# Order of the mixers' small matrix products on TensorE, in a two-layer hybrid encoder

## Chip, cores and metric

The kernel runs on one core of one Trainium2 chip. The metric is the device time of one execution in microseconds (us), as the median of several runs. Each profile is one execution taken by the hardware profiler.

## What is computed

The input x is 512 tokens of 1024 features in float32. Two layers follow each other; each adds half a SwiGLU feed-forward block, a token mixer, and again half a feed-forward block, each behind an RMS norm. The mixer computes four branches from one projection of the normalised input, weighs them with sigmoid gates and projects the sum:

```python
p = u @ w_in
p_da, p_gla, p_ssd, p_rw, p_gate = split_cols(p, MIXER_COLS)
...   # A: differential attention, 4 heads x 2 score maps, 64 wide
y_a = differential_attention(q, k, v, lam, lam_init, da_norm)
...   # B: gated linear attention, 4 heads, chunks of 64 tokens
o = gla_chunked(q, k, v, log_g)
...   # C: Mamba-2 SSD, 8 heads, 2 groups, chunks of 64 tokens
y = ssd_chunked(xh, dt, A, bm, cm) + ssd_d[:, None] * xh
...   # D: RWKV-7, 8 heads of 64, a state of 64 x 64 per head
state = state * w_t + sa[..., None] * (kk_t * a_t) + v_t[..., None] * k_t
...
proj = jnp.einsum('bsnc,ncd->bsnd', ys, w_branch)
merged = jnp.sum(sigmoid(p_gate + gate_b) * proj, axis=2)
return merged @ w_out
```

## The kernel before

**Wide products.** Projections, feed-forward, gates, merges and output are products of 128 rows, 128 columns and 512 moving columns. Each is made of three float32r products of split operands (high x high, high x low, low x high): `mm3` at L164 to L166, `tok` at L201 to L203. A weight unit comes by a DMA on SP's queue into one of three buffers, and ScalarE and VectorE split it (L157, L159).

**The mixer.** `cotrace` traces two streams against each other, by estimated costs that the streams yield as (TensorE time, latency after it). One is RWKV-7 (`rwkv`); the other is attention (`diff_attn`), then `gla`, then `ssd`. Where TensorE would idle by the estimate, it traces filler: the 32 gates, then the merges of branches that are done. From the traced order, as priorities, and the dependencies a scheduler makes a fixed order for each engine. Every engine then works through its queue in that order.

**Small products.** The mixers' own products are float32. Their operands lie on 128, 64 or 32 partitions (the rows of the array), and their outputs on 128, 64 or 32 partitions (its columns). Chunks have 64 tokens, and a 128-partition tile holds two heads or two chunks, one in partitions 0 to 63 and one in 64 to 127. The lines that matter:
- L615 (`rwkv`, preparation): the chunk's 128 x 128 interaction matrices of one head, 64 rows, four chunks to an output tile; heads one after the other, each with its own "rs" tile, and VectorE's masking (through the helper at L81) behind each.
- L651: the products of those matrices with v, 64 x 64, eight chunks of one head, then of the other.
- L705 and L709: the 32 x 32 corrections of the triangular inverses, again head by head, with a negation on ScalarE (L707) between them.
- L735, L743, L749, L757 to L763: the chunk recurrence, four products each (two head pairs, two heads). A PSUM tile `step` holds all of a chunk's. The last two kinds share an accumulation and are kept in order by `chained`:

```python
last = self.chained(last, lambda: mm(
    out=o, lhsT=am[pl, h, hf][:, cc, 64:128], rhs=sav[hf][:, pl, cc, h, :], start=True, stop=c == 0))
if c:
    last = self.chained(last, lambda: mm(
        out=o, lhsT=ar[pl, hf][hp, cc, 1, :], rhs=state[hp, pl, :], start=False, stop=True))
```

- L719 turns the normalised output of a chunk pair, with heads in turn.
- L518 and L522: two projections of RWKV's low-rank parts, from partitions 0 to 63 and 64 to 127.
- L871 (`diff_attn`): the scores of one of a head's two maps, 64 rows, up to 512 keys; VectorE masks and reduces each before the next is traced. L885 and L891 are the transposes and the product with v.
- L1025 and L1031 (`gla`): per chunk four products with the state and four that make the next state; after each of the latter VectorE updates the state (L1033, L1035) from the same PSUM tile.
- L1154, L1163, L1168 (`ssd`): the products within the chunk (two chunks of a token tile one after the other), the products with the state, and those for the next state.

**PSUM.** `small(tag)` hands out tiles of one bank; the tags "pb", "rs", "os" and "oy" have two banks each. RWKV uses "rs", the other mixers "os", and "oy" for some outputs and for `tok`.

Of the kernel before, what the change touches and what calls it, by code (L numbers as in the profile page):

```python
# [73 lines left out]
class Body:  # L74
# [4 lines left out]
    # ---------------------------------------------------------------- helpers  # L79
# [22 lines left out]
    def rsqrt(self, y, a, pool, tag):  # L102
        """y = a ** -0.5 for normal positive a."""
# [14 lines left out]
    def rsqrt_neg_half(self, hm, pool):  # L118
        """a ** -0.5 for the [128, 1] tile hm = -a / 2."""
# [3 lines left out]
        # the shifted sign and the halved exponent are in the constant  # L123
# [6 lines left out]
    def keep(self, t):  # L130
        """0 at the chunks' starts, 1 elsewhere."""
        self.nc.gpsimd.memset(t, 1.0)
        self.nc.gpsimd.memset(t[:, 0:512:64], 0.0)
        return t

    @contextmanager
    def prio(self, d):
        """Issue what is traced within as if it were traced d instructions later."""
        self.tc.cur_priority += d
        yield  # L140
        self.tc.cur_priority -= d

    def chained(self, last, fn):
        """Issue the matmuls that fn traces behind the matmul last (order in one PSUM bank)."""
        if last is None:
            return fn()
        with self.tc.issue_after(last.ins):
            return fn()

    # ------------------------------------------------------------ weight units  # L150
# [17 lines left out]
    def feat(self, ap):  # L168
        """[128 features, 512 tokens] of the projection by one unit."""
# [7 lines left out]
    def feat2(self, aps):  # L177
        """Two units' projections, the first half of the tokens before the second."""
# [12 lines left out]
    def tok(self, units, lh, ll, tags=("pb", "pb", "oy", "oy"), tail=0):  # L191
        """Four [128 tokens, 512] products: stationary lh/ll (feature-major), moving the units.
        The last tail units go by token tile, so that the tiles end one after another."""
# [27 lines left out]
    # ------------------------------------------------------------------ norm  # L221
# [9 lines left out]
    def norm_(self, x, gain, pool, out=None, g=None):  # L231
        """RMS norm of x (tiles [t][half]); to xh/xl feature-major, or rows to out."""
# [6 lines left out]
        for t in range(NT):  # L239
            # hm = -(mean square + eps) / 2, the first half's part ahead of the second's  # L240
# [38 lines left out]
    # ------------------------------------------------------------------- ffn  # L279
# [26 lines left out]
    # ----------------------------------------------------------------- mixer  # L306
# [65 lines left out]
    def filler(self, yd, gd, es):  # L372
        """The gates, then the merges of the branches that are done."""
# [38 lines left out]
    def cotrace(self, streams, filler):  # L412
        """Trace the streams by their estimated times, the filler where TensorE would idle."""
# [52 lines left out]
    # ---------------------------------------------------------------- RWKV-7  # L466
    def rwkv(self, ydst):
# [34 lines left out]
        for ph in range(2):  # L502
# [5 lines left out]
            for pl in range(2):  # L508
# [26 lines left out]
                # decay of the state between the chunks' references  # L535
# [12 lines left out]
                # normalised key  # L548
# [20 lines left out]
                # k' = k (1 + (a - 1) k_a)  # L569
# [3 lines left out]
                # bonus  # L573
# [17 lines left out]
                for hf in range(2):  # L591
# [6 lines left out]
                    # rows of even heads hold [beta | kappa], of odd ones [kappa | beta]  # L598
# [12 lines left out]
                    for h in range(2):  # L611
                        hp = slice(64 * h, 64 * h + 64)
                        ps = self.small("rs", (128, 4, 128))
                        for j in range(4):
                            mm(  # L615
                                out=ps[:, j, :],
# [4 lines left out]
                            )  # L621
                        m = r2((128, 4, 128), name="am")
                        self.mul(m, ps, self.c("rwmask").unsqueeze(1).to_broadcast([128, 4, 128]))
# [9 lines left out]
                # v token-major: even heads on partitions 64..127, odd ones on 0..63  # L633
# [12 lines left out]
                # A(kappa, alpha) V  # L646
                pu = self.small("rs", (128, 8, 64))
                for h in range(2):
                    hp, vp = slice(64 * h, 64 * h + 64), slice(64 - 64 * h, 128 - 64 * h)
                    for c in range(NC):  # L650
# [7 lines left out]
            # inverses of the unit-triangular 32x32 diagonal blocks, a block per partition  # L658
# [39 lines left out]
            for pl in range(2):  # L698
# [3 lines left out]
                for h in range(2):  # L702
                    lo, hi = slice(64 * h, 64 * h + 32), slice(64 * h + 32, 64 * h + 64)
                    for c in range(NC):
                        mm(out=ps[hi, c, :], lhsT=am[pl, h, c // 4][lo, c % 4, 32:64], rhs=xt1[pl][lo, c, :],  # L705
                           start=True, stop=True)
                    self.act(qt[hi], ps[hi], AF.Copy, scale=-1.0)  # L707
                    for c in range(NC):
                        mm(out=ps2[lo, c, :], lhsT=qt[hi, c, :], rhs=tt[pl][hi, c, 32:64], start=True, stop=True)  # L709
                    nc.vector.tensor_copy(tt[pl][lo, :, 32:64], ps2[lo])  # L710
# [14 lines left out]
            # the chunks in turn  # L725
            state, late = None, None
            for c in range(NC):
# [19 lines left out]
                if c < NC - 1:  # L747
# [7 lines left out]
                    else:  # L755
                        self.mul(new, step[:, 2], fc)
                for pl, h, hp in heads:  # L757
# [584 lines left out]
```

## Time and profile before

| | |
|---|---|
| median of 3 runs | 3215.84 us (3211.01 to 3217.59) |
| span of the profiled execution | 3212.2 us, 40884 instructions |
| TensorE busy | 3147.8 us (98%) |
| weight loads busy (beside the matmuls) | 2499.3 us (78%) |
| VectorE busy | 1621.3 us (50%) |
| ScalarE busy | 1148.1 us (36%) |
| granted clock of TensorE over the span | 0.991 of full speed |

The busy time of an engine is the time in which at least one of its instructions runs. Matmuls are pipelined and their ends are modelled: a busy TensorE isn't one at its peak, and the time that one product costs is read from its start and the start of the next.

### The profile page before, as it was taken

The numbers are of one execution on the slowest core, as the hardware profiler recorded it, in microseconds if no ns is written. First come the engines' busy times: TensorE is split into PE (matmuls) and PEld (weight loads), VectorE is DVE, ScalarE is ACT, GpSimd is POOL, SyncE is SP. The second block draws the span as 40 slices with busy tenths as digits, with TensorE's granted clock in tenths as the row PEclk, the third lists the DMA queues.
The fourth block names the chain that finished last, engine by engine and source line by source line (L and its number), as shares of the span: only waits on it lengthen the run. The fifth ranks groups of instructions, "written<-read, shape, count | busy, mean of one in ns | idle before, by whom it ended". The sixth has DMA issues, their size and how long they took to land.

```text
span 3212.2 us, 40884 instructions
## 1 busy us (share of the span) xinstructions
PE 3147.8 (98%) x16160; PEld 2499.3 (78%) x16160; DVE 1621.3 (50%) x3310; ACT 1148.1 (36%) x1754; POOL 137.8 (4%) x160
## 2 busy tenths in 40 slices
PE   8999999999999999999999999999999999999998
PEld 6888787777777777888888888777777777778887
DVE  4332446756475775332343324567654757753323
ACT  3222245654432323222222223356553323232222
POOL 0000000000011100000000000000000011000000
PEclk9999999999999999999999999999999999999999
DMA  4222322322222543222332233223122215432222
GB/s 165 98 98 93 129 89 88 103 67 96 86 83 63 180 168 138 99 98 93 108 132 94 99 112 110 93 87 104 60 93 95 86 56 181 172 132 93 98 99 79
DMA packets 138592, 338.50 MB, mean 105 GB/s; under 512 B 35104, under 2 KB 43680, under 8 KB 137632
## 3 DMA queue, kind: packets, MB, share of 16 engines
q1 hardware_dynamic: 138400, 335.88, 30.8%
q8 instruction: 127, 2.08, 0.3%
q14 instruction: 65, 0.53, 0.1%
HBM read 297.55 MB, written 38.27 MB: 105 GB/s over the span
## 4 chain that ended last, share of the span: by engine, by line
PE 90%; DVE 7%; ACT 2%; issue 1%; DMA 0%; SPq 0%; DVEq 0%; ACTq 0%
PE pb L164 18%; PE pb L165 18%; PE pb L166 18%; PE oy L203 3%; PE oy L201 3%; PE oy L202 3%; PE pb L202 2%; PE pb L201 2%; PE pb L203 2%; PE rs L203 1%; PE os L203 1%; PE rs L201 1%; PE os L201 1%; PE os L202 1%; PE rs L202 1%; PE os L871 1%
## 5 line engine op out<-in xcount | busy, mean ns | idle before, releaser
L157 ACT CAST whi<-wraw 128x1024 fp32r<-128x1024 f32 x478 | 501.6, 1051 | 1479.6 <-PE pb L165 545.8
L159 DVE TENSOR_TENSOR wlo<-wraw,whi 128x1024 fp32r<-128x1024 f32 x466 | 571.7, 1227 | 894.5 <-ACT whi L157 880.8
L164 PE MATMUL pb<-xh,whi 128*128 128x512 f32 (+1 forms) x2448 | 957.0, 391 | 4.9 <-DVE rwr L97 2.7
L165 PE MATMUL pb<-xl,whi 128*128 128x512 f32 (+1 forms) x2448 | 949.5, 388 | 3.4 <-DVE xl L81 3.4
L166 PE MATMUL pb<-xh,wlo 128*128 128x512 f32 (+1 forms) x2448 | 949.6, 388 | 0.0
L164 PEld LDWEIGHTS pb<-xh,whi 128*128 128x128 f32 x2448 | 466.5, 191 | 110.2 <-issue 16.6
L165 PEld LDWEIGHTS pb<-xl,whi 128*128 128x128 f32 x2448 | 466.7, 191 | 95.8 <-issue 6.3
L166 PEld LDWEIGHTS pb<-xh,wlo 128*128 128x128 f32 x2448 | 467.0, 191 | 93.5 <-issue 6.1
L81 DVE TENSOR_TENSOR s<-s,pb 128x512 f32<-128x512 f32 x88 | 60.5, 688 | 286.9 <-PE pb L166 284.8
L100 ACT ACT_TABLE_LOAD x118 | 151.4, 1283 | 12.5 <-PE os L1141 9.7
L165 PE MATMUL pb<-yl,whi 128*128 128x512 f32 x256 | 102.1, 399 | 0.9 <-DVE yl L81 0.9
L164 PE MATMUL pb<-yh,whi 128*128 128x512 f32 x256 | 102.5, 403 | 0.0
L166 PE MATMUL pb<-yh,wlo 128*128 128x512 f32 x256 | 102.1, 399 | 0.0
L159 POOL TENSOR_TENSOR wlo<-wraw,whi 128x1024 fp32r<-128x1024 f32 x12 | 28.4, 2379 | 1318.3 <-ACT whi L157 1318.3
L202 PE MATMUL pb<-wlo,xh 128*128 128x512 f32 x192 | 76.7, 399 | 0.0
L201 PE MATMUL pb<-whi,xh 128*128 128x512 f32 x192 | 76.6, 399 | 0.0
L201 PE MATMUL oy<-whi,xh 128*128 128x512 f32 x192 | 76.0, 396 | 0.0
L203 PE MATMUL oy<-whi,xl 128*128 128x512 f32 x192 | 75.8, 395 | 0.0
L203 PE MATMUL pb<-whi,xl 128*128 128x512 f32 x192 | 75.8, 395 | 0.0
L202 PE MATMUL oy<-wlo,xh 128*128 128x512 f32 x192 | 75.3, 392 | 0.0
L201 PE MATMUL pb<-whi,hh 128*128 128x512 f32 x176 | 69.1, 392 | 0.0
L202 PE MATMUL pb<-wlo,hh 128*128 128x512 f32 x176 | 69.0, 392 | 0.0
(418 smaller groups left out, 4339.7 us busy)
## 6 DMA issues: line engine op xcount, KB each, us to landing
wraw<-in_ffn_gu SPq DMA_DIRECT2D x176, 512.0 KB, 3.2
wraw<-in_win_f SPq DMA_DIRECT2D x118, 512.0 KB, 3.3
wraw<-in_ffn_d SPq DMA_DIRECT2D x88, 512.0 KB, 3.2
wraw<-in_win_t SPq DMA_DIRECT2D x48, 512.0 KB, 3.3
gd<-sg SPq DMA_DIRECT2D x64, 256.0 KB, 2.1
wraw<-in_wbr SPq DMA_DIRECT2D x32, 512.0 KB, 3.4
msg<-gd SPq DMA_DIRECT2D x64, 256.0 KB, 3.0
wraw<-in_wout SPq DMA_DIRECT2D x16, 512.0 KB, 3.2
```

Of the source, the lines that this page charges most:

```text
L81: return (eng or self.nc.vector).tensor_tensor(out=out, in0=in0, in1=in1, op=op)
L100: return self.nc.scalar.activation(out=out, in_=in_, func=func, **kw)
L157: nc.scalar.copy(hi, raw)
L159: eng.tensor_tensor(out=low, in0=raw, in1=hi.bitcast(F32), op=ALU.subtract)
L164: mm(out=ps, lhsT=lh, rhs=rh, start=first, stop=False)
L165: mm(out=ps, lhsT=lh, rhs=rl, start=False, stop=False)
L166: return mm(out=ps, lhsT=ll, rhs=rh, start=False, stop=last)
L201: mm(out=pst[t], lhsT=lh(k)[:, lt], rhs=hi[:, c], start=k == 0, stop=False)
L202: mm(out=pst[t], lhsT=lh(k)[:, lt], rhs=low[:, c], start=False, stop=False)
L203: mm(out=pst[t], lhsT=ll(k)[:, lt], rhs=hi[:, c], start=False, stop=k == nk - 1)
L871: mm(out=s[:, 0:n], lhsT=qT[qb][cp_, h, :], rhs=kT[h][cp_, 0:n], start=True, stop=True)
```

## The change

In the mixers, loops around small products change places: products that lie next to each other in the traced order now use different halves of the array's rows or columns (two heads or two chunks in turn), and products of one shape are traced as a group. For that, L615 and the scores of L871 take two PSUM tiles at once, and the scores move from tag "os" to "oy". GLA goes by token tiles of two chunks, makes all products for the state first, then the updates, and then the products with the state; its yields change accordingly. SSD makes both chunks' products for the state, then the states, then the products with them. In the chunk recurrence the first group of products sets the start flag only for the first head pair of the tile. No operation is added or removed. Comments go, so later lines have other numbers.

```diff
-                    for h in range(2):
-                        hp = slice(64 * h, 64 * h + 64)
-                        ps = self.small("rs", (128, 4, 128))
-                        for j in range(4):
+
+                    pss = [self.small("rs", (128, 4, 128)) for _ in range(2)]
+                    for j in range(4):
+                        for h in range(2):
+                            hp = slice(64 * h, 64 * h + 64)
                             mm(
-                                out=ps[:, j, :],
+                                out=pss[h][:, j, :],
                                 lhsT=b[hp, j].rearrange("p s t -> p (s t)"),
                                 rhs=x[hp, j].rearrange("p s t -> p (s t)"),
                                 start=True,
                                 stop=True,
                             )
+                    for h in range(2):
                         m = r2((128, 4, 128), name="am")
-                        self.mul(m, ps, self.c("rwmask").unsqueeze(1).to_broadcast([128, 4, 128]))
+                        self.mul(m, pss[h], self.c("rwmask").unsqueeze(1).to_broadcast([128, 4, 128]))
...
-                for h in range(2):
-                    hp, vp = slice(64 * h, 64 * h + 64), slice(64 - 64 * h, 128 - 64 * h)
-                    for c in range(NC):
+                for c in range(NC):
+                    for h in range(2):
+                        hp, vp = slice(64 * h, 64 * h + 64), slice(64 - 64 * h, 128 - 64 * h)
                         mm(out=pu[hp, c, :], lhsT=am[pl, h, c // 4][vp, c % 4, 0:64],
                            rhs=sav[c // 4][vp, pl, c % 4, h, :], start=True, stop=True)
...
                 qt = r2((128, 8, 32), name="qt")
-                for h in range(2):
-                    lo, hi = slice(64 * h, 64 * h + 32), slice(64 * h + 32, 64 * h + 64)
-                    for c in range(NC):
+                los = [slice(64 * h, 64 * h + 32) for h in range(2)]
+                his = [slice(64 * h + 32, 64 * h + 64) for h in range(2)]
+                for c in range(NC):
+                    for h, (lo, hi) in enumerate(zip(los, his)):
                         mm(out=ps[hi, c, :], lhsT=am[pl, h, c // 4][lo, c % 4, 32:64], rhs=xt1[pl][lo, c, :],
                            start=True, stop=True)
+                for hi in his:
                     self.act(qt[hi], ps[hi], AF.Copy, scale=-1.0)
-                    for c in range(NC):
+                for c in range(NC):
+                    for lo, hi in zip(los, his):
                         mm(out=ps2[lo, c, :], lhsT=qt[hi, c, :], rhs=tt[pl][hi, c, 32:64], start=True, stop=True)
+                for lo in los:
                     nc.vector.tensor_copy(tt[pl][lo, :, 32:64], ps2[lo])
...
                 for pl, h, hp in heads:
-                    o = step[hp, 3, pl, :]
                     last = self.chained(last, lambda: mm(
-                        out=o, lhsT=am[pl, h, hf][:, cc, 64:128], rhs=sav[hf][:, pl, cc, h, :], start=True, stop=c == 0))
-                    if c:
+                        out=step[hp, 3, pl, :], lhsT=am[pl, h, hf][:, cc, 64:128], rhs=sav[hf][:, pl, cc, h, :],
+                        start=pl == 0, stop=c == 0, skip_group_check=True))
+                if c:
+                    for pl, h, hp in heads:
                         last = self.chained(last, lambda: mm(
-                            out=o, lhsT=ar[pl, hf][hp, cc, 1, :], rhs=state[hp, pl, :], start=False, stop=True))
+                            out=step[hp, 3, pl, :], lhsT=ar[pl, hf][hp, cc, 1, :], rhs=state[hp, pl, :],
+                            start=False, stop=True, skip_group_check=True))
...
+                sc = [self.small("oy") for _ in range(2)]
                 for c in range(2):
-                    s = self.small("os")
                     cp_ = slice(64 * c, 64 * c + 64)
-                    mm(out=s[:, 0:n], lhsT=qT[qb][cp_, h, :], rhs=kT[h][cp_, 0:n], start=True, stop=True)
+                    mm(out=sc[c][:, 0:n], lhsT=qT[qb][cp_, h, :], rhs=kT[h][cp_, 0:n], start=True, stop=True)
+                for c, s in enumerate(sc):
...
-        for c in range(NC):
-            t, j = c // 2, c % 2
-            b = slice(64 * j, 64 * j + 64)
-            if j == 0:
-                psy = self.small("oy", (128, 4, 128))
-            for q in range(4):
-                mm(out=psy[b, q, :], lhsT=lq[q][:, c, :], rhs=rv[c][:, q, :], start=True, stop=True)
-            if c < NC - 1:
-                pk = self.small("os", (128, 2, 128))
+        for t in range(NT):
+
+            n = 2 if t < NT - 1 else 1
+            pk = self.small("os", (128, 2, 2, 128))
+            for j in range(n):
                 for q in range(4):
                     p, h = q // 2, q % 2
                     hp, vp = slice(64 * h, 64 * h + 64), slice(64 - 64 * h, 128 - 64 * h)
-                    mm(out=pk[hp, p, :], lhsT=kd[p][vp, c, :], rhs=rv[c][vp, q, :], start=True, stop=True)
+                    c = 2 * t + j
+                    mm(out=pk[hp, j, p, :], lhsT=kd[p][vp, c, :], rhs=rv[c][vp, q, :], start=True, stop=True)
+            for j in range(n):
+                c = 2 * t + j
+                for q in range(4):
+                    p, h = q // 2, q % 2
+                    hp = slice(64 * h, 64 * h + 64)
                     if c == 0:
-                        nc.vector.tensor_copy(rv[1][hp, q, :], pk[hp, p, :])
+                        nc.vector.tensor_copy(rv[1][hp, q, :], pk[hp, j, p, :])
                     else:
-                        self.stt(rv[c + 1][hp, q, :], rv[c][hp, q, :], dec[p][hp, c : c + 1], pk[hp, p, :], ALU.mult, ALU.add)
...
+                        self.stt(rv[c + 1][hp, q, :], rv[c][hp, q, :], dec[p][hp, c : c + 1], pk[hp, j, p, :], ALU.mult, ALU.add)
+            psy = self.small("oy", (128, 4, 128))
+            for q in range(4):
+                for j in range(2):
+                    c = 2 * t + j
+                    mm(out=psy[64 * j : 64 * j + 64, q, :], lhsT=lq[q][:, c, :], rhs=rv[c][:, q, :], start=True, stop=True)
...
+            yield 1.4, 3.5
...
-            for j in range(2):
-                b = slice(64 * j, 64 * j + 64)
-                for h in range(8):
+            for h in range(8):
+                for j in range(2):
+                    b = slice(64 * j, 64 * j + 64)
                     mm(out=py1[b, h, :], lhsT=lm[b, h, :], rhs=xc[b, h, :], start=True, stop=True)
             self.add(yi, py1, xd)
+            phs = [self.small("oy", (128, 8, 64)) for _ in range(2 if t < NT - 1 else 1)]
+            for g in range(2):
+                for j, ph in enumerate(phs):
+                    b = slice(64 * j, 64 * j + 64)
+                    mm(out=ph[:, 4 * g : 4 * g + 4, :].rearrange("p h f -> p (h f)"), lhsT=bt[b, g, :],
+                       rhs=xe[b, 4 * g : 4 * g + 4, :].rearrange("p h f -> p (h f)"), start=True, stop=True)
+            states = [state]
+            for j, ph in enumerate(phs):
+                c = 2 * t + j
+                new = self.g2((128, 8, 64), name="hs")
+                if c == 0:
+                    nc.scalar.copy(new, ph)
+                else:
+                    self.mul(new, state, dc[:, c, :].unsqueeze(2).to_broadcast([128, 8, 64]), nc.gpsimd)
+                    self.add(new, new, ph)
+                state = new
+                states.append(new)
             py2 = self.small("os", (128, 8, 64))
-            for j in range(2):
-                c = 2 * t + j
-                b = slice(64 * j, 64 * j + 64)
-                cs = slice(c * 64, c * 64 + 64)
-                if c:
-                    for g in range(2):
-                        mm(out=py2[b, 4 * g : 4 * g + 4, :].rearrange("p h f -> p (h f)"), lhsT=cf[g][:, cs],
-                           rhs=state[:, 4 * g : 4 * g + 4, :].rearrange("p h f -> p (h f)"), start=True, stop=True)
-                if c < NC - 1:
-                    ph = self.small("oy", (128, 8, 64))
-                    for g in range(2):
-                        mm(out=ph[:, 4 * g : 4 * g + 4, :].rearrange("p h f -> p (h f)"), lhsT=bt[b, g, :],
-                           rhs=xe[b, 4 * g : 4 * g + 4, :].rearrange("p h f -> p (h f)"), start=True, stop=True)
-                    new = self.g2((128, 8, 64), name="hs")
-                    if c == 0:
-                        nc.scalar.copy(new, ph)
-                    else:
-                        self.mul(new, state, dc[:, c, :].unsqueeze(2).to_broadcast([128, 8, 64]), nc.gpsimd)
-                        self.add(new, new, ph)
-                    state = new
+            for g in range(2):
+                for j in range(2):
+                    if states[j] is not None:
+                        cs = slice((2 * t + j) * 64, (2 * t + j) * 64 + 64)
+                        mm(out=py2[64 * j : 64 * j + 64, 4 * g : 4 * g + 4, :].rearrange("p h f -> p (h f)"), lhsT=cf[g][:, cs],
+                           rhs=states[j][:, 4 * g : 4 * g + 4, :].rearrange("p h f -> p (h f)"), start=True, stop=True)
```

## Rows read from the trace of the kernel before

**Rows 1.** The page's part 4: shares of the chain that ended last.

```profile
PE 90%; DVE 7%; ACT 2%; issue 1%; DMA 0%; SPq 0%; DVEq 0%; ACTq 0%
```

**Rows 2.** Stretches, both mixers: length, busy us (instructions) per engine, clock, DMA.

```profile
394.00:1237.00 843.00, 833.52 (x4732) 632.84 (x4730) 532.33 (x1280) 362.67 (x595) 55.83 (x70) 1.00 0.31 104
...
1988.00:2838.00 850.00, 837.94 (x4732) 635.87 (x4732) 534.36 (x1275) 362.69 (x595) 57.73 (x70) 0.99 0.31 103
```

**Rows 3.** TensorE in order of time: start, us to modelled end, line, tiles, count.

```profile
666.12 1.12 PE L871 MATMUL os<-kT,qT 64*128 64x512 f32 x2
667.17 0.33 PE L759 MATMUL rs<-sav,am 128*64 128x64 f32 x2
667.43 0.33 PE L762 MATMUL rs<-st,ar 64*64 64x64 f32 x2
...
669.22 0.50 PE L166 MATMUL pb<-xh,wlo 128*128 128x512 f32 x1
...
671.75 0.45 PE L719 MATMUL rs<-ident,yc 64*64 64x64 f32 x8
672.04 0.40 PE L735 MATMUL rs<-st,ar 64*64 64x64 f32 x8
```

**Rows 4.** The same view around chunk 0 of a head group.

```profile
654.39 0.45 PE L759 MATMUL rs<-sav,am 128*64 128x64 f32 x8
654.77 0.45 PE L735 MATMUL rs<-st,ar 64*64 64x64 f32 x8
655.15 0.50 PE L164 MATMUL pb<-xh,whi 128*128 128x512 f32 x1
```

**Rows 5.** The same view, RWKV's preparation.

```profile
889.63 1.90 PE L615 MATMUL rs<-ar,bkf 64*128 64x128 f32 x16
891.46 0.43 PE L1031 MATMUL os<-rv,ax 64*64 64x128 f32 x2
```

**Rows 6.** The same view, two projections from opposite row halves.

```profile
863.55 0.69 PE L518 MATMUL rs<-rwa,lor 64*128 64x512 f32 x1
863.56 0.69 PE L522 MATMUL rs<-rwa,lor 64*128 64x512 f32 x1
...
864.61 1.09 PE L1025 MATMUL oy<-rv,lq 128*64 128x128 f32 x8
```

**Rows 7.** The same view, GLA's chunks.

```profile
908.51 0.44 PE L1031 MATMUL os<-rv,ax 64*64 64x128 f32 x4
908.88 0.43 PE L1025 MATMUL oy<-rv,lq 128*64 128x128 f32 x2
909.24 0.50 PE L165 MATMUL pb<-xl,whi 128*128 128x512 f32 x1
...
912.01 0.50 PE L166 MATMUL pb<-xh,wlo 128*128 128x512 f32 x1
912.45 0.43 PE L1031 MATMUL os<-rv,ax 64*64 64x128 f32 x2
912.80 0.43 PE L1025 MATMUL oy<-rv,lq 128*64 128x128 f32 x2
```

**Rows 8.** The same view, SSD.

```profile
1046.96 1.90 PE L1154 MATMUL oy<-xc,lm 64*64 64x64 f32 x32
1048.78 1.13 PE L1168 MATMUL oy<-xe,bt 64*128 64x256 f32 x4
1049.84 0.50 PE L164 MATMUL pb<-xh,whi 128*128 128x512 f32 x1
```

**Rows 9.** The same view, 32 x 32 products.

```profile
637.35 0.69 PE L705 MATMUL rs<-xt,am 32*32 32x32 f32 x16
637.96 1.12 PE L871 MATMUL os<-kT,qT 64*128 64x512 f32 x2
```

**Rows 10.** VectorE's groups: shapes, count, busy us, mean ns, idle before, releasers.

```profile
L81 DVE TENSOR_TENSOR am<-rs,cst 128x512 f32<-128x512 f32 x32 | 22.0, 689 | 23.8 <-PE rs L615 23.5
```

More of the change, by code (lines that the diff above doesn't have):

```diff
@@ L1032, in gla @@
                     if c == 0:
-                        nc.vector.tensor_copy(rv[1][hp, q, :], pk[hp, p, :])
+                        nc.vector.tensor_copy(rv[1][hp, q, :], pk[hp, j, p, :])
                     else:
-                        self.stt(rv[c + 1][hp, q, :], rv[c][hp, q, :], dec[p][hp, c : c + 1], pk[hp, p, :], ALU.mult, ALU.add)
-            if j == 1:
-                sq = self.g2((128, 4, 128), name="gsq")
-                y3 = psy
-                self.act(sq, y3, AF.Square)
-                ss = cp.tile([128, 4], F32, tag="gs", bufs=2, name="gs")
-                nc.vector.tensor_reduce(out=ss, in_=sq, axis=AX.X, op=ALU.add)
-                self.ts(ss, ss, 1.0 / 128, ALU.mult, EPS, ALU.add)
-                rs = cp.tile([128, 4], F32, tag="gr", bufs=2, name="gr")
-                self.rsqrt(rs, ss, cp, "gl")
-                self.mul(sq, y3, rs.unsqueeze(2).to_broadcast([128, 4, 128]))
-                s = og[t]
-                self.mul(s, s, sq.rearrange("p h v -> p (h v)"))
-                pt = self.small("os", (128, 4, 128))
-                for h in range(4):
-                    nc.tensor.transpose(pt[:, h, :], s[:, h * 128 : (h + 1) * 128], self.ident)
-                self.act(sq, pt, AF.Identity, scale=self.p("gla_n"))
-                nc.sync.dma_start(out=ydst[:, :, t * 128 : (t + 1) * 128], in_=sq)
@@ L1053, in gla @@
-            yield 0.8, 1.75
+                        self.stt(rv[c + 1][hp, q, :], rv[c][hp, q, :], dec[p][hp, c : c + 1], pk[hp, j, p, :], ALU.mult, ALU.add)
[4 more added lines that the diff above has]
+                    mm(out=psy[64 * j : 64 * j + 64, q, :], lhsT=lq[q][:, c, :], rhs=rv[c][:, q, :], start=True, stop=True)
+            sq = self.g2((128, 4, 128), name="gsq")
+            y3 = psy
@@ new lines, in gla @@
+            self.act(sq, y3, AF.Square)
+            ss = cp.tile([128, 4], F32, tag="gs", bufs=2, name="gs")
+            nc.vector.tensor_reduce(out=ss, in_=sq, axis=AX.X, op=ALU.add)
+            self.ts(ss, ss, 1.0 / 128, ALU.mult, EPS, ALU.add)
+            rs = cp.tile([128, 4], F32, tag="gr", bufs=2, name="gr")
+            self.rsqrt(rs, ss, cp, "gl")
+            self.mul(sq, y3, rs.unsqueeze(2).to_broadcast([128, 4, 128]))
+            s = og[t]
+            self.mul(s, s, sq.rearrange("p h v -> p (h v)"))
@@ L1056, in ssd @@
+            pt = self.small("os", (128, 4, 128))
+            for h in range(4):
+                nc.tensor.transpose(pt[:, h, :], s[:, h * 128 : (h + 1) * 128], self.ident)
+            self.act(sq, pt, AF.Identity, scale=self.p("gla_n"))
+            nc.sync.dma_start(out=ydst[:, :, t * 128 : (t + 1) * 128], in_=sq)
+            yield 1.4, 3.5
     def ssd(self):
```

## The prediction

> **What bounds the kernel now.** I read the chain of waits on the page first: TensorE holds 90% of it, VectorE 7% [rows 1]. Then the table of stretches: the change touches the mixer alone, which runs once per layer, from 394 to 1237 and from 1988 to 2838 us; there TensorE is busy 834 of 843 and 838 of 850 us, VectorE 532 and 534, ScalarE 363 [rows 2]. So in the mixer nothing but TensorE's own time counts, as long as other work is ready to fill it. Busy time doesn't tell what an instruction costs, though, because the ends of matmuls are modelled and overlap. So the third view is the order in time on TensorE alone, where I read distances between starts, not durations. A product of two float32 operands shows there as two instructions ("x2"), one of float32r operands as one.
>
> Four things are to be seen there.
> 1. *Alternating shapes.* In a chunk step of RWKV, L759 (128 rows, 64 columns) and L762 (64, 64) alternate product by product. The eight products go from 667.17 to 669.22: 2.05 us, 0.26 each [rows 3]. In chunk 0, where L762 is absent, the four L759 stand together and take 0.38 us; four L735, of L762's shape with heads alternating, take 0.38 too, what it costs to leave the shape included [rows 4], and four L719 take 0.29 [rows 3].
> 2. *Halves.* L518 reads rows 0 to 63 and L522 rows 64 to 127. They start 0.01 us apart, and both products of 512 columns are through after 1.06 us [rows 6]; one L871 of that size takes 1.05 us alone [rows 3]. The second half is free. It is so for columns too: L759's heads differ in columns alone.
> 3. *Runs on one half.* Eight L615 of one head and then eight instructions of the other take 1.83 us, 0.11 from start to start [rows 5]; 32 instructions of L1154, sixteen on each half in turn, take 1.82 us, 0.057 each [rows 8]; heads alternating, L719 takes 0.036 [rows 3].
> 4. *Breaks.* A single wide product between two small ones takes 0.44 us [rows 7], ten in a row 2.53 us, 0.25 each [rows 3]. So each break of the wide stream costs 0.2 us.
>
> **The change part by part.** Nothing is computed more or less; every instruction stays, in another order. Counts are from the loops, for both layers.
>
> *A, chunk steps (L756 to L763).* 2 layers x 2 head groups x 7 chunks = 28 places. 2.05 becomes 0.38 (a run like chunk 0's L759) and 0.38 (a run like L735): 28 x 1.29 = 36 us. Should the halves not overlap, each run would take 0.61 (eight starts of 0.057 and 0.15 to leave): 28 x 0.83 = 23. I take 36, since rows 4 are the same operands and positions.
>
> *B, L615.* 16 places (2 layers x 4 head pairs x 2 halves of the chunks). 1.83 becomes eight starts of 0.11 and 0.2 to enter and leave, 1.1: 16 x 0.73 = 12. Where the two runs stand apart now, up to 1.0 is saved (16 us); if heads only partly meet, 6. I take 13.
>
> *C, attention scores (L871).* 32 pairs. At 512 keys a pair goes from 2.10 to 1.06; with 384, 256 and 128 keys I scale this down, so 0.63 as the mean and 20 us at most; some at 128 keys overlap already, so 18. Low end 10.
>
> *D, L651 and L1154.* Eight runs of 32 each. 1.82 becomes sixteen starts of 0.057 and 0.15: 1.08. Sixteen runs x 0.74 = 12; low end 6, because heads of L651 already overlap in places.
>
> *E, L705 and L709.* 32x32 products, 0.61 per 16 [rows 9], 32 such runs. If a pair takes the time of one start, 16 x 0.6 = 10 us are saved; no row shows a long run of pairs so small, so the ends are 0 and 10, and I take 6, as pairs of every other shape overlap.
>
> *F, GLA (L1025, L1031).* Now each L1031 is followed by VectorE's read of the same PSUM tile (L1033 and the line of the state update, L1035), which parts it from the next. One L1031 or L1025 costs 0.36, two L1031 that meet 0.37 together [rows 7]. 56 and 64 products alone would be 43 us; in runs of eight (eight starts of 0.11 and 0.25, 1.1 us each, 15 full runs' worth) 17 us. Some stand in runs already, so I take 20 rather than 26; low end 12. They also break the wide stream: from 864 to 933 us I count 25 breaks between them (rows 7 show one), where eight runs need ten at most, so 15 fewer in a layer: 30 x 0.2 = 6 us (0 to 10).
>
> *G, SSD (L1163, L1168).* Two L1168 of one half take 1.06 [rows 8]; four of both halves will take that. Three token tiles in four have both halves, so 6 x 1.06 = 6, and as much for L1163, which has the same 256 columns: 12; low end 6.
>
> The sum is 36 + 13 + 18 + 12 + 6 + 20 + 6 + 12 = 123 us.
>
> *What it adds.* (i) L615 takes both "rs" buffers at once and the scores both "oy" buffers (before, the scores shared "os" with the transposes and the P.V products). TensorE's queue is in order: if the second buffer is late, the wide products behind wait too. What frees an "rs" is mostly VectorE's masking, 0.69 us [rows 10]. (ii) ScalarE's negations of L707 wait for all of L705, GLA's L1025 for the state updates of two chunks, SSD's L1163 for both states; VectorE's first masking for four products more. All these are under 2 us, and wide products stand between producer and consumer now (ten after 669.22). (iii) The 0.5 us by which the first masking slips also holds two small stores on SP's queue, with weight loads behind them; three weight buffers cover that. (iv) In SSD the second chunk's state product needs the "oy" that L1155's addition of py1 frees. I take 8 of the 123 us off for pairs that other work still parts and for such waits; if the cover is gone at all 54 places of (i) and (iv), 54 x 0.69 = 37 us.
>
> The profiled execution's span is 3212.2 us and the median of the runs 3215.8, so 3.6 lie around it or are spread. 3212.2 - 115 + 3.6 = 3101.
>
> **A rule that speaks against it.** L719's heads read different rows and write different halves of the partitions of one PSUM bank, and eight instructions take 0.29 us [rows 3], half of what L1154 needs on one half [rows 8]. The Trainium skill, "TensorEngine Tiling (Array Packing)", section "Restrictions and Gotchas", says that different row tiles cannot access the same PSUM bank simultaneously; by that, L651, L1154, L705, L709, L762 and L1031 would gain nothing from taking turns, and the time would be the third rival's below. The trace does not bear that out for halves that write different partitions.
>
> **The rivals.**
> - *The mixer runs out of filler.* With TensorE done sooner, the two streams' chains of VectorE and ScalarE steps become the bound, and half of the gain comes back as idle time: 3216 - 58 = 3158. For it: VectorE is at 63% there [rows 2], with waits in order. Against it: TensorE idles only 9 to 12 us per mixer, and the merges and gates are there to be pulled forward.
> - *The pairs are not neighbours when issued,* so that the change does half of what it says: shapes are grouped, halves don't overlap. A 23, the breaks 6, F 4: 33 us, 3183. Against it: rows 4 and 6 show traced neighbours issued as neighbours.
> - *One bank, no overlap.* Halves that write the same PSUM bank may have to take turns where VectorE reads that bank soon, unlike L719's. Then D, E, half of L1031's 10 and, in A, 0.23 x 28 are lost: 12 + 6 + 5 + 6 = 29 of 115; 3130.
> - *Slower: two buffers at once.* At the 16 places of B, the 32 of C and the 6 of G, TensorE's queue stands until the second buffer is free. It decides from 115/54 = 2.1 us per place; at 3 us, 162 are lost and 3263 results. VectorE would have to be several maskings behind (0.69 each) [rows 10]; against it is that it waits for L615 before the masking in most places, 23.8 us in all [rows 10].
>
> **How the numbers follow.** Forecast 0.74; filler 0.09; not neighbours 0.05; one bank 0.08; slower 0.04. Predicted is the first, 3101. Low end: the high terms 36 + 16 + 20 + 12 + 10 + 26 + 10 + 12 = 142, and some 8 of waits that grouping may remove: 3066. High end: the low terms 23 + 6 + 10 + 6 + 0 + 12 + 0 + 6 = 63: 3153, which takes in the one-bank case; I go on to 3158, where filler lies, because without it over 2 in 10 would be left out. A measurement of this kernel can tell 0.2%, 6 us, from no change. Faster by more than that is 0.93, with every case but slower and a part of "not neighbours"; same 0.03; slower 0.04.
>
> **What would show it.** In the order in time after the change: runs of eight L759 and eight L762 of 0.4 us each; L615's sixteen in 1.1 us; score pairs starting 0.01 us apart and through in 1.06; L1031 in runs of sixteen. The FFN stretches should not move, and each mixer be some 57 us shorter at the same idle time. I am wrong if a mixer shrinks less than its runs do (idle TensorE: filler or buffers), if starts within a run stay at 0.057 or 0.11 (no overlap), or if wide products still part the pairs.

## The result and the profile after

The changed kernel takes 3165.72 us (median of 4 runs, 3164.53 to 3169.1) against 3215.35 for the kernel before, with one run more than the table above has: a ratio of 0.9847, 95% interval 0.9833 to 0.9862. It is 50 us faster; 3101 had been predicted, 115 us faster, with 3158 as the upper end. The profiled span fell from 3212.2 to 3162.7 us, by 49.5.

By the page after, TensorE is busy for 3071.4 us (97%), VectorE for 1627.7 (51%) and ScalarE for 1137.3 (36%). Its part 4 (shares of the chain that ended last):

```profile
PE 86%; DVE 10%; ACT 3%; issue 1%; DMA 0%; SPq 0%; DVEq 0%; ACTq 0%
```

TensorE's share of the chain fell from 90% to 86%, and VectorE and ScalarE took the 4 points [rows 1]. Both mixers, from behind the norm's first transposes to the next norm's wait, with the columns of [rows 2]:

```profile
394.00:1212.00 818.00, 796.81 (x4742) 605.25 (x4741) 534.83 (x1283) 356.99 (x593) 52.33 (x69) 0.99 0.34 108
1968.00:2784.00 816.00, 794.90 (x4690) 602.01 (x4689) 531.58 (x1270) 355.00 (x589) 52.00 (x69) 0.99 0.33 106
```

TensorE is idle for 21 us in each mixer, where it was 9.5 and 12 [rows 2] (8 in each, if the wait at the next norm is left out there too). So a part of the gain came back as idle time. The order in time on TensorE shows the rest. First what came as forecast: a pair of scores at 384 keys, a chunk step, a GLA group, and SSD's products within the chunk.

```profile
582.14 0.92 PE L880 MATMUL oy<-kT,qT 64*128 64x384 f32 x4
582.99 0.66 PE L638 MATMUL rs<-ident,rwv 128*128 128x128 f32 x4
...
657.22 0.45 PE L765 MATMUL rs<-sav,am 128*64 128x64 f32 x8
657.60 0.45 PE L770 MATMUL rs<-st,ar 64*64 64x64 f32 x8
658.05 1.16 PE L901 MATMUL os<-dv,dap 128*128 128x128 f32 x8
...
874.92 1.09 PE L1038 MATMUL os<-rv,ax 64*64 64x128 f32 x16
...
1058.24 1.15 PE L1170 MATMUL oy<-xc,lm 64*64 64x64 f32 x32
1059.32 1.13 PE L1176 MATMUL oy<-xe,bt 64*128 64x256 f32 x4
```

The two scores of 384 keys (L880, L871 before) are through after 0.85 us, 0.42 each. L765 and L770 (L759 and L762) take 0.83 us together where they alternated for 2.05 [rows 3]; L1170 (L1154) takes 1.08 us where it took 1.82 [rows 8]. Then what did not:

```profile
646.52 1.12 PE L880 MATMUL oy<-kT,qT 64*128 64x512 f32 x2
647.58 0.45 PE L749 MATMUL rs<-un,tt 64*64 64x64 f32 x8
...
649.04 1.12 PE L880 MATMUL oy<-kT,qT 64*128 64x512 f32 x2
650.10 0.45 PE L755 MATMUL rs<-sav,bk 128*64 128x64 f32 x8
...
878.75 1.90 PE L616 MATMUL rs<-ar,bkf 64*128 64x128 f32 x16
880.58 1.09 PE L1052 MATMUL oy<-rv,lq 128*64 128x128 f32 x16
...
1060.38 0.65 PE L1194 MATMUL os<-hs,conv 128*64 128x256 f32 x2
...
1061.62 1.13 PE L1176 MATMUL oy<-xe,bt 64*128 64x256 f32 x4
```

At 512 keys the two scores of a pair stand 2.5 us apart with other work between, each alone for 1.06 us, as before; six of the eight pairs of that size are parted like this. Sixteen L616 (L615) take 1.83 us, exactly what they took [rows 5]. And four L1176 (L1168) take 1.06 us, as before [rows 8], with the other chunk's four 2.3 us later.

To see how much each part gave, I charge each TensorE instruction with the time from its start to the next start, less any idle time in between, and add these up over both layers, before and after (us). The idle time is a row of its own: all that TensorE has but the waits for the norms at L256, which are the same in both profiles (24.7 and 24.8).

| part | before | after | saved | forecast |
|---|---|---|---|---|
| A chunk steps, L765 L770 | 57.3 | 22.4 | 34.9 | 36 |
| B L616 | 32.4 | 31.0 | 1.4 | 13 |
| C scores, L880 | 41.1 | 30.5 | 10.6 | 18 |
| D L653, L1170 | 30.9 | 19.9 | 11.0 | 12 |
| E L708, L714 | 17.7 | 11.9 | 5.8 | 6 |
| F GLA, L1038 L1052 | 37.9 | 19.8 | 18.1 | 20 |
| G SSD, L1176 L1194 | 29.6 | 26.7 | 2.9 | 12 |
| A to G | 246.9 | 162.2 | 84.6 | 117 |
| wide products (419 and 423 unbroken stretches) | 2711.6 | 2719.7 | -8.1 | 6 (fewer breaks) |
| TensorE idle | 19.1 | 45.3 | -26.2 | -8 |

So 32 us of the 117 weren't saved, the wide products took 8 us more instead of 6 less, and idle time took 18 us more than allowed: 32 + 14 + 18 = 64 of the 65 us that are missing. Some expectations below count the idle time behind a product in: with it G is 31.5 after, and B saved 2.6.

Where the idle time sits, the waits of TensorE in the kernel after show (instruction waited at, what it waited for: us in total, times, longest):

```profile
PE pb L165 <- DVE yl L81: 9.3, 8, 1.9
...
PE pb L164 <- ACT yh L383: 3.7, 4, 0.9
...
PE pb L164 <- ACT yh L1220: 3.0, 2, 1.5
```

"yh" and "yl" are the high and low part of a finished branch's output, the operands of its merge. Each mixer's merges begin once, behind the gates, and change from one branch to the next three times; at each of these four places TensorE now stands. The second of them in layer 1, from attention's merge to RWKV's, in order of time on TensorE, then on ScalarE and VectorE:

```profile
1074.55 0.60 PE L1214 MATMUL os<-ident,xd 128*128 128x128 f32 x4
1074.99 0.60 PE L1139 MATMUL os<-ident,conv 128*128 128x128 f32 x4
1076.10 0.44 PE L1147 MATMUL os<-ident,conv 128*128 128x128 f32 x2 [0.51 <-DVE sz L81]
1077.46 0.73 PE L164 MATMUL pb<-yh,whi 128*128 128x512 f32 x2 [0.93 <-ACT yh L383]
1078.03 0.40 PE L1157 MATMUL os<-rr,gtbd 128*128 128x512 f32 x1
1078.36 0.65 PE L1194 MATMUL os<-hs,conv 128*64 128x256 f32 x2
1079.79 0.50 PE L165 MATMUL pb<-yl,whi 128*128 128x512 f32 x1 [0.79 <-DVE yl L81]
```

```profile
1075.52 1.89 ACT L383 CAST yh<-y 128x2048 fp32r<-128x2048 f32 x1
...
1077.44 2.29 DVE L81 TENSOR_TENSOR yl<-y,yh 128x2048 fp32r<-128x2048 f32 x1 [0.21 <-ACT yh L383]
```

The previous merge's last product starts at 1074.32. Only then is a pair of split buffers free (there are two; SSD's own output, split tile by tile, holds the other), and ScalarE first ends the split of a weight that it began at 1074.56; so the cast of 1.89 us and the subtraction of 2.29 us come late and one after the other, and from 1074.55 to 1079.79 TensorE has 13 small instructions and two of the merge. It idles 2.23 us there; the four places of the layer cost 2.24, 2.23, 2.58 and 2.38. In the kernel before, the same change:

```profile
1105.68 1.90 PE L1154 MATMUL oy<-xc,lm 64*64 64x64 f32 x32
1107.51 0.65 PE L1163 MATMUL os<-hs,conv 128*64 128x256 f32 x2
1108.09 1.13 PE L1168 MATMUL oy<-xe,bt 64*128 64x256 f32 x4
1109.14 0.73 PE L164 MATMUL pb<-yh,whi 128*128 128x512 f32 x2
1109.81 1.13 PE L1168 MATMUL oy<-xe,bt 64*128 64x256 f32 x4
1110.86 0.51 PE L165 MATMUL pb<-yl,whi 128*128 128x512 f32 x1
```

The slow, unpaired SSD products lay over the split and hid it: idle 0, 0, 0.47 and 0 us at the four places. So 2 x (9.43 - 0.47) = 18 of the 26 us of new idle time lie there, 13 of them at the first three. RWKV's last product now starts 28 us sooner (1032.9 where it was 1061.3), the merges begin sooner, and the changes fall elsewhere in SSD: here on its transposes (L1214, L1139, L1147), before on its products.

### The profile page after: what moved, and what is told of

It reads as the page before. It is cut to its first block, busy times and chain, and to the rows that moved or that the text cites. A ratio compares the mean times of both kernels' runs of the same rounds, so it can differ in the third digit from the quotient of the medians.

```text
span 3162.7 us, 40871 instructions
## 1 busy us (share of the span) xinstructions
PE 3071.4 (97%) x16160; PEld 2440.9 (77%) x16160; DVE 1627.7 (51%) x3310; ACT 1137.3 (36%) x1746; POOL 133.8 (4%) x160
## 4 chain that ended last, share of the span: by engine, by line
PE 86%; DVE 10%; ACT 3%; issue 1%; DMA 0%; SPq 0%; DVEq 0%; ACTq 0%
PE pb L165 18%; PE pb L164 17%; PE pb L166 17%; PE oy L201 3%; PE oy L203 3%; PE oy L202 3%; PE pb L201 2%; PE pb L203 2%; PE pb L202 2%; PE os L202 1%; PE rs L202 1%; PE rs L203 1%; PE os L203 1%; PE rs L201 1%; PE os L201 1%
## 5 line engine op out<-in xcount | busy, mean ns | idle before, releaser
L165 PEld LDWEIGHTS pb<-yl,whi 128*128 128x128 f32 x256 | 49.7, 194 | 25.8 <-DVE yl L81 12.8
L256 PE MATMUL os<-ident,xn 128*128 128x128 f32 x192 | 34.9, 315 | 35.7 <-DVE xn L97 35.7
```

The costliest lines, as they stand in the source:

```text
L165: mm(out=ps, lhsT=lh, rhs=rl, start=False, stop=False)
L256: nc.tensor.transpose(ps[:, k, :], xn[h][:, k * 128 : (k + 1) * 128], self.ident)
```

## The experiments

**The chunk steps alone** (the kernel before, with part A only).

```diff
-                    if c:
+                if c:
+                    for pl, h, hp in heads:
                         last = self.chained(last, lambda: mm(
```

> The kernel before (3215.4 us) with the chunk steps alone changed: four products of L759, then four of L762. Theory 'what the blocks lose the kernel gains': 28 places x 1.25 to 1.29 us, 35 us less: 3180 us (3177 to 3185). Rival 'given back': the gain in the head group's chunk loop is lost where the shorter products no longer cover other waits; a third or more is missing: 3190 us or more.

Measured: ratio 0.986 (0.9845 to 0.9875), 3172.28 us. Part A fell by 35.4 us, as forecast. The span fell by 42.7, so that the time is 5 us under the expected range; 16 us fewer at half clock, some 7 us of time by the price in the last section, go with the rest. This one edit has nearly all of the time that the whole change brings. But its four runs have a granted clock of 0.993 to 0.994 of full speed, the changed kernel's 0.989 to 0.991; at 0.3% of the time, that is some 10 us, so the other edits may give more than the 7 us between the medians.

**RWKV's parts alone** (the kernel before, with A, B, E and L653).

```diff
+                    pss = [self.small("rs", (128, 4, 128)) for _ in range(2)]
...
+                for c in range(NC):
+                    for h in range(2):
...
+                if c:
+                    for pl, h, hp in heads:
```

> The kernel before (3217 us) with all of RWKV's changes (chunk steps, L615, L651, L705, L709) and nothing in the other mixers. The chunk steps alone gave 0.9860. By the starts, the rest of RWKV saves 2.6 (L615) + 4.7 (L651) + 5.7 (L705, L709) = 13 us. Theory 'what the blocks lose the kernel gains': 0.982, 3159 us. Rival 'given back': 0.985 to 0.988, 3168 to 3178, at 10 us or more of new idle time.

Measured: 0.9856 (0.9841 to 0.9872), 3170.36 us, no different from A alone. The small products (those that don't use the whole array) fell by another 8 us, but the wide ones rose by 3, idle time by 3 and the other products by 2; the time at half clock went from 42.3 back to 58.6 us. So it isn't the 10 us of new idle time that the rival named.

**L616's products in turn** (the changed kernel; `chained` keeps them in the traced order).

```diff
+                    turn = None
                     for j in range(4):
                         for h in range(2):
-                            mm(
+                            turn = self.chained(turn, lambda: mm(
```

> The changed kernel (3165.7 us) with the eight products of L616 (L615 before) issued strictly in turn between the two heads, by the same means that keeps the chunk steps' products in order. Theory 'not neighbours when issued': in the changed kernel the scheduler issues four products of one head, then four of the other, because the second PSUM buffer comes free later; in turn, 16 instructions take 1.1 to 1.3 us instead of 1.8 to 1.9, at 16 places: 8 to 12 us less, 3155 us (3152 to 3160). Rival 'row halves of 128 columns don't overlap in runs': the block stays at 1.8 us and the time at 3166. Rival 'the second buffer is late': the block is shorter but the wide products behind it wait, and the time is 3166 to 3175.

Measured: 0.9815 (0.98 to 0.983), 3157.79 us, as the theory had it; the intervals don't overlap. L616 fell from 31.0 to 23.8 us, and the profiled spans, at nearly the same time at half clock (61.2 and 59.6 us), differ by 5.7. In order of time (the line is 617 here):

```profile
509.16 0.49 PE L617 MATMUL rs<-ar,bkf 64*128 64x128 f32 x2
509.47 0.48 PE L881 MATMUL oy<-kT,qT 64*128 64x128 f32 x4
509.89 0.49 PE L164 MATMUL pb<-xh,whi 128*128 128x512 f32 x1
510.31 1.16 PE L617 MATMUL rs<-ar,bkf 64*128 64x128 f32 x14
511.40 0.50 PE L165 MATMUL pb<-xl,whi 128*128 128x512 f32 x1
```

Fourteen now take 1.09 us, 0.078 from start to start instead of 0.114. So the halves do overlap for this shape; the changed kernel didn't issue them as neighbours. One product still goes ahead alone at all 16 places; that the second "rs" is late there fits, but no run took it by itself.

**SSD's states as before** (the changed kernel without G).

```diff
-            phs = [self.small("oy", (128, 8, 64)) for _ in range(2 if t < NT - 1 else 1)]
-            for g in range(2):
-                for j, ph in enumerate(phs):
...
+            for j in range(2):
...
+                    ph = self.small("oy", (128, 8, 64))
```

> The changed kernel (3165.7 us) with the SSD's products for the next state and with the state (L1163, L1168 before) in the order of the kernel before; only the products within the chunk stay paired. Theory 'no pairs there': those lines took 29.6 us before and 31.5 after, so nothing is lost: 3162 to 3167 by the sum. Theory 'lost cover' adds that these products again stand where one merge ends and the next begins, and takes off some of the 14 us idle there: 3155 to 3163. Rival 'the SSD pairs pay': 12 us were predicted for them; then it is slower, 3172 to 3178.

Measured: 0.9855 (0.9837 to 0.9873), 3171.8 us; the interval holds the change's 0.9847. G gives nothing that can be measured. This profile has 78.3 us at half clock against 61.2, some 7 us of time, so not even the sign of its 6 us is G's. Idle time stayed as well (45.9 us): the old order alone doesn't cover the changes of merge again.

**The scores as before** (the changed kernel without C).

```diff
-                sc = [self.small("oy") for _ in range(2)]
                 for c in range(2):
+                    s = self.small("os")
...
-                for c, s in enumerate(sc):
```

> The changed kernel (3165.7 us, 0.9847) with the attention scores as before: one product at a time, in the 'os' buffers. The scores' starts took 41.1 us before and 30.5 in the changed kernel. Theory 'what the blocks lose the kernel gains': 10 us slower, 0.988, 3176 us. Rival 'given back': what the pairs of scores save comes back as waits later in the mixer, and the time stays at 3162 to 3169.

Measured: 0.9852 (0.9834 to 0.987), 3169.55 us. Undoing C cost the small products 11.9 us (231.5 to 243.4), but the time only 4, inside the intervals: in the profile idle time fell by 3.5 us and the wide products by 4.5. Of the runs with a granted clock of 0.991, this kernel's took 3165.03 us, the changed kernel's 3164.53 and 3164.84.

**Three split buffers** (the changed kernel; a third pair of yh and yl).

```diff
-        return [self.mp.tile([128, 4, 512], F32R, tag=t, bufs=2, name=t) for t in ("yh", "yl")]
+        return [self.mp.tile([128, 4, 512], F32R, tag=t, bufs=3, name=t) for t in ("yh", "yl")]
...
-                        outs.append([lp.tile([128, 4, 512], F32R, name=n) for n in ("ah", "al")] if d else self.y_split())
+                        outs.append(self.y_split())
```

> The changed kernel (3165.7 us) with three instead of two buffers for the split outputs of a branch (yh, yl), so that the next branch's can be loaded and split while the last one's merge still runs; the place comes from the split copy of the second half of the merged sum, which takes one of the three. Nothing else differs. Theory 'lost cover': at the three changes from one branch's merge to the next in each layer, TensorE stands 2.2 to 2.6 us (six times, 14 us), because the shorter and better paired SSD products no longer lie there; with a third buffer this idle time goes: 3152 us, 3148 to 3157, and TensorE's wait for yl falls from 9.3 us to under 2. Rival 'VectorE is the bound after RWKV': splitting and adding take it 77 to 84% there, so earlier loads change nothing: 3163 to 3168.

Measured: 0.9778 (0.9758 to 0.9798), 3145.31 us, the fastest of all and 7 us under what was expected. The second of the four places, on TensorE, then on ScalarE and VectorE:

```profile
1050.58 0.39 PE L164 MATMUL pb<-yh,whi 128*128 128x512 f32 x1
1050.81 0.40 PE L165 MATMUL pb<-yl,whi 128*128 128x512 f32 x1
```

```profile
1050.69 1.91 ACT L383 CAST yh<-y 128x2048 fp32r<-128x2048 f32 x1 [3.29 <-DMA y<-yd]
1052.63 2.29 DVE L81 TENSOR_TENSOR yl<-y,yh 128x2048 fp32r<-128x2048 f32 x1 [1.87 <-ACT yh L383]
```

The split now runs beside a merge that still goes on, and the second and third places have no idle time. The first keeps its 2.24 us, as the first output is loaded only when RWKV's tiles are given up, and the fourth, which waits for SSD's own output, has 2.55. In the span (18.6 us less), idle time makes 9.3. The small products take what they took; the rest is in the wide products (5 us) and the other ones, and 12.4 us fewer are at half clock, some 5 us of time.

**GLA as before** (the changed kernel without F).

```diff
-        for t in range(NT):
+        for c in range(NC):
+            t, j = c // 2, c % 2
...
-            for q in range(4):
-                for j in range(2):
...
-            yield 1.4, 3.5
```

> The changed kernel (3165.7 us, 0.9847) with the gated linear attention as before, chunk by chunk. Its products' starts took 37.9 us before and 19.8 in the changed kernel. Theory 'what the blocks lose the kernel gains': 18 us slower, 0.990, 3183 us. Rival 'given back': the time stays at 3162 to 3172, because the stretch behind RWKV then has its small products where the merges change again.

Measured: 0.9823 (0.9806 to 0.984), 3160.82 us: undoing F, which had saved 18 us of products, cost nothing; by the medians it is 5 us faster, but the intervals overlap. Small products rose by 21.5 us, idle time fell by 19 (45.3 to 26.3): the changes of merge are covered again, with 0, 0.27, 1.63 and 0 us of idle time.

**A third pair without the change, and with GLA as before** (the edit of three split buffers, on two other kernels). If the third pair were a gain of its own, it would give about the same 20 us wherever it is put.

> The kernel before with a third pair of yh/yl buffers and nothing of the change (the merge of layer 2 takes its operands from the same three buffers). Theory 'lost cover': in the kernel before SSD's small products lie at each change of merge, and TensorE is idle there 0.5 us per layer at most, so the third pair has almost nothing to cover: 3206 to 3218 us, within 0.3% of before, and idle time in the mixers stays near 19 us. Rival, 'a third pair is a gain of its own' (the merge units can be laid anywhere, with or without the change): about the 20 us that it gave behind the change, 3190 to 3200.

> The change with GLA as before (chunk by chunk) and a third pair of yh/yl buffers. Theory 'lost cover': GLA as before already covers two of the three changes of merge, so the third pair saves only what is left there, some 4 us, and the pairs in GLA, which now cost no cover, are missed with some 17 us of small products: 3154 to 3160, slower than three buffers behind the whole change (3145). Rival, 'GLA's order costs in itself' (its yields and its longer groups disturb the filler, not only the cover): the third pair gives its 20 us here too, 3138 to 3145, the fastest so far.

Measured: 0.9982 (0.997 to 0.9994) and 3210.43 us on the kernel before; 0.9807 (0.9789 to 0.9825) and 3154.56 us with GLA as before. The third pair is worth 0.2%, 6 us, where the changes of merge were covered, and there it left the idle time as it was (19.1 and 19.3 us), with 7 us fewer at half clock; it is worth 6 us with GLA as before, and 20 in the changed kernel. So it mends what the change opened. With the third pair, F is worth 9 us by the medians (3154.6 to 3145.3), where without it it gave nothing; the intervals still touch.

**Both mends at once** (three split buffers and L616 in turn).

```diff
+                            turn = self.chained(turn, lambda: mm(
...
+        return [self.mp.tile([128, 4, 512], F32R, tag=t, bufs=3, name=t) for t in ("yh", "yl")]
```

> The changed kernel (3165.7 us) with both mends: three buffers for the split outputs and L616 in strict turn between the heads. Alone, the first gave 0.9778 and the second 0.9815 of the kernel before, against 0.9847 for the change. Theory 'two separate causes' (the merges' changes in the stretch behind RWKV, pairs parted by late buffers in RWKV's preparation): both gains add, 0.975, 3137 us (3132 to 3143). Rival 'one resource': the second gain is only idle time moved into the stretch behind RWKV, and the two don't add: 0.978, 3146 to 3150 us.

Measured: 0.9787 (0.9772 to 0.9802), 3148.48 us: the gains, 20 and 8, don't add. The waits of TensorE show a new one, which the kernel with the third pair alone doesn't have:

```profile
PE oy L1171 <- DVE lm L81: 5.5, 2, 2.8
```

SSD's products within the chunk wait for VectorE's decay matrix. L616 in turn alone has the same wait of 5.5 us, so it comes with the turns. But it stands at the first of the four places, where TensorE otherwise waited 1.89 us in each layer for the split, and idle time as a whole is only 0.8 us more than with the third pair alone (36.8 and 36.0). So it isn't what eats the gain. The profile has 64.5 us at half clock against 48.8, some 7 of the 11 us that are missing; why, and the other 4, is not settled.

## Why the prediction was wrong

**What held.** The price of an instruction was read rightly from starts: A 34.9 (36), D 11.0 (12), E 5.8 (6) and F 18.1 (20), together 70 of 74 us, with values from runs as short as [rows 4] and, for E, from the overlap of other shapes. (One reading was too high: 0.29 us for eight L719 is not half of what L1154 needs on one half, but 0.036 against 0.057, some two thirds; no term used it.) The rival of one bank didn't come: L1170's halves write one bank, and 32 instructions take 1.08 us, 0.034 each. The Trainium skill ("TensorEngine Tiling (Array Packing)", "Restrictions and Gotchas") states that different row tiles cannot access one PSUM bank at the same time; this row doesn't bear that out for halves that write different partitions. The slower rival (two buffers at once) didn't come as a standing queue: TensorE's waits at L616 are 2.8 us in all.

**Step B and G, and half of C: pairs that the code traces aren't pairs that the engine gets.** The forecast named this rival and held it off with rows 4 and 6, "traced neighbours issued as neighbours". But those rows are of products that share one tile, or (L518, L522) of two tiles that didn't part them. B, C and G take two PSUM tiles at once, and (i) asked only whether TensorE's queue would stand until the second is free. It doesn't: the scheduler, which makes the order with the dependencies known, issues the first half's products and the other half's later. That is a third outcome, neither overlap nor wait, and its price is the gain: B 12 us, G 9, C 7. For B the chained order shows by experiment that the parting costs it: 7.2 of the missing us came back. For C, the pairs of 512 keys are those that save most (1.06 us); 6 of the 8 are parted, which makes 6.4 us, while all pairs of 384 keys overlap. For G it is read from the order in time alone, and no run tried to mend it. That the second tile is free too late for the scheduler is the reading that fits all three, but no run freed one sooner.

**The breaks.** GLA's groups were to save 30 breaks. Its L1038 do stand in runs of sixteen, and the breaks that hold a GLA product fell from 50 to 32. But the wide stream is broken 423 times, before 419: 22 breaks came at other products. A break belongs to the whole order, and the step counted it as GLA's own. The wide products take 8 us more, not 6 less; four breaks at 0.2 us are 1 of these, 3 us more at half clock another 1, and the rest stays open.

**The term for waits, and the filler rival.** 8 us were taken off for pairs still parted and for waits at the edited lines; 26 us of new idle time came, 18 of them where the merges begin or change, in lines that the change leaves alone for the most part. The rival "the mixer runs out of filler" had half of the gain come back as idle time, and its 3158 us is nearer to the result than 3101. But it isn't quite what happened: 26 us of idle time came, not 58, and not because filler ran out, but because filler wasn't ready. The merges' split (1.9 + 2.3 us, with a buffer that comes free only when the previous merge ends) had been hidden by slow small products, and the change made exactly these faster and moved the merges away from them. The prediction did not name what the removed time had covered: 34, 37 and 25 small instructions start within the first three splits before, 10, 5 and 5 after. The runs with a third pair and those with GLA as before show it from several sides: the pair takes the idle time away at two places where it had come, and changes none where there was cover. About half of the third pair's 20 us is idle time; how the rest divides between the clock (last section) and the order is not separated.

**What stays open.** The other 8 us of new idle time are spread over waits of some 2 us at most, and no run took them one by one; nor did one take away the wait for SSD's own output at the fourth place. That RWKV's other parts and C bring nothing that can be measured by themselves is shown; that the clock and the places of the fillers take it back is argued from sums of one profile each.

## What to carry to other kernels

Work that is slow on the bound engine may be the cover for something else: before shortening it, list what other engines do during it, and what they must deliver at its end. A pair that needs two buffers can be parted when the order is made, so look at the order that came out and at what frees the second, or fix the order by hand; here the pairs inside one tile came without that. And when several edits are tried together, each needs its own run: here one edit of a few lines has nearly all of the gain, one seems to count only with a third buffer, and one does nothing that can be measured.

## What the hardware showed beside that

A few short idle times can be followed by a stretch at the lower of TensorE's two clocks. At the second of the four places in layer 2, where TensorE waits 0.51, 0.93 and 0.78 us within 4 us, the stretches are (columns as in [rows 2]; the last three are the granted clock, the DMA share and GB/s):

```profile
2644.00:2646.20 2.20, 1.42 (x6) 0.55 (x6) 2.20 (x2) 0.49 (x2) 0.00 (x0) 1.00 0.00 0
2646.20:2649.60 3.40, 3.40 (x9) 2.63 (x10) 3.40 (x4) 0.21 (x1) 1.43 (x1) 0.50 0.66 241
2649.60:2653.00 3.40, 3.40 (x16) 2.75 (x15) 2.29 (x4) 0.39 (x1) 0.00 (x0) 1.00 0.61 227
```

For 3.40 us the granted clock is 0.50, 1.2 GHz, and the stretch holds 9 instructions instead of the 16 of the next, at 1.00: a loss of some 1.5 us, two thirds of the idle time itself. The same place in layer 1, with the same waits, isn't followed by such a stretch. In total the profiles hold between 42.3 us (chunk steps alone) and 78.3 us (SSD's states as before) at half clock, 58.3 before and 61.2 after; at 1.5 us lost in 3.4, that spread of 36 us is 16 us of time. Differences of 5 to 8 us between two of these kernels can therefore be the clock, and nothing follows from them alone; of the 8 us of L616 in turn, 5.7 are there between two profiles with nearly the same time at half clock (59.6 and 61.2). Why one kernel has less of it than another is open.
